# A hybrid encoder layer on one core: the layout of attention's queries, keys and outputs in DRAM

## The chip, the cores and the metric

The kernel runs on one core of a Trainium2 chip. Time is the device time of one execution in microseconds (us); the median of several runs counts. Beside the timed runs there is one profiled execution, from which every row shown here comes. Its engines: TensorE (PE) multiplies matrices, VectorE (DVE) and ScalarE (ACT) work on rows of 128 partitions, GpSimd (POOL) takes a few small operations and the accumulating transfers, SyncE (SP) issues all other transfers. A transfer (DMA) is moved by up to 16 transfer engines that all queues share.

## The reference

One layer over x (1024 frames of width 1024, float32). One projection gives queries, keys and values for attention (8 heads of 64), forget gates, the inputs of a gated linear recurrence (4 heads of 128) and two sets of merge gates. Then:

```python
y_a = fox_attention(q_a, k_a, v_a, log_fa)      # causal softmax(q k^T / 8 + F[t] - F[s]) v
y_b = rmsnorm(hgrn2_chunkwise(...)) * sigmoid(g_b)
merged = sigmoid(gate_a) * (y_a @ w_pa) + sigmoid(gate_b) * (y_b @ w_pb)
x = layer_norm(ALPHA * x + merged @ w_o)
x = layer_norm(ALPHA * x + (silu(g) * u) @ w_ff_out)   # u, g = split(x @ w_ff_in)
```

## The kernel before

**Precision and products.** A float32 operand is split into a high part (a cast to the fast type of TensorE) and a low part (the remainder). A product is three matmuls of these parts (`mm3`), each 128x128 by 128x512 as a rule. Most weight products are done two by two in Strassen's way: 7 block products in place of 8, with sums of blocks made on VectorE.

**Stages, in the order of time.** First the value projections and the forget gates (to about 90 us of the span). Then the steps in `ORDER`: "b" are pairs of projections for the recurrence, "q0" to "q3" make the queries and keys of two heads each (`qk_pair`), "r" are the recurrence's heads (`hgrn`), "e" and "g" the early and late parts of the merge gates (`gate_early`, `gate_late`), "a0" to "a7" the attention heads. Then the branch projections, the output projection, the first normalisation, the FFN in 22 chunks, and the second normalisation.

**Queries, keys and outputs on their way through DRAM.** `qk_pair` has a pair of heads in 128 partitions (64 of head 2p, 64 of head 2p+1) and stores four halves of them, high and low, in `qk_d[p, n]`: n = 0, 1 are the high and low parts of the queries, 2 and 3 those of the keys. There are 32 such stores of 128 rows of 2 KB. `qk_load` fetches what one head needs into three tiles of 128 partitions: `q2` holds the high queries in the upper 64 partitions and the low ones in the lower 64, `k2` the high keys twice, `kl` the low keys twice. A score is then two matmuls, `q2` with `k2` and `q2` with `kl`. Each tile is filled by two transfers of 64 rows of 4 KB, 48 in all. `attention` multiplies the probabilities with values that stand as high and low parts beside each other, so its result has the two parts' products in 2 x 64 partitions; it is stored in `ya_d[p, i]` (pair p, head i of it, part a), 16 stores. `branch_raw` brings the outputs of a pair of heads into one tile of 128 partitions: for each head a load of the first part by SyncE, and on it an accumulating transfer of the second part by GpSimd, 8 of each, 64 rows of 4 KB.

**Buffers.** Tiles are taken by tag; a tag has a fixed number of buffers, handed on in order. `ybox[0]` (the raw outputs) and `ybox[1]` (their sums for Strassen's products) take the tags "v" and "m", which before are the wide boxes of probabilities (`wide`) of the odd and the even heads, and later the two halves of the merged rows (`mraw`).

**What sets the order of the work.** All instructions are first recorded and then placed by a planner (`Plan`). It knows a cost for each operation (`cost`) and dependencies by tiles and by ranges of DRAM, simulates the engines and the transfers, and tries 36 variations of due times, of which it keeps the order with the earliest end. Each engine then runs its own instructions in that fixed order; so every constant of the planner can move instructions all over the kernel. For transfers it counts bytes at 235, 220 or 350 bytes per ns (64 rows, broadcast rows, others). An accumulating transfer is counted apart: it lands `LANDS` ns + bytes / `RATE` after its issue, and keeps the transfer engines for half of bytes / `RATE`. At most `RING` of them are under way.

Every operation is issued through one line of the planner (line 391), so the profile tells groups apart by tile names and not by lines. Names in rows: `qk_d`, `ya_d`, `part_d`, `gate_d` are in DRAM; `yboxv` is the raw outputs' tile and `yboxm` that of their sums before the change.

Of the kernel before, what the change touches and what calls it, by code (L numbers as in the profile page):

```python
# [7 lines left out]
F32 = mybir.dt.float32  # L8
# [4 lines left out]
ALU = mybir.AluOpType  # L13
# [3 lines left out]
P = 128  # L17
S = 1024
# [3 lines left out]
HA, DH = 8, 64  # L22
# [8 lines left out]
FIRST = 8  # L31
WARM = 7
ROUNDS = 36
ORDER = ("b10 00", "b20 21", "b11 01", "r0", "q0", "b12 02", "r1", "b22 23", "q1", "r2", "b13 03", "q2", "e0", "r3", "q3", "e1",
         "e2", "e3", "e4", "e5", "e6", "e7", "a0", "a1", "g0", "a2", "a3", "g1", "a4", "g2", "a5", "a6", "g3", "a7", "g4", "g5", "g6", "g7")
MARGIN = 1.06
SLACK = 400.0
SWITCH = 300.0
# [23 lines left out]
class Plan:  # L62
# [2 lines left out]

    LAT = {"PE": 197.0, "ACT": 131.0, "DVE": 128.0, "POOL": 66.0, "SP": 2400.0}
    OWN = {"PE": 0.0, "ACT": 0.0, "DVE": 127.0, "POOL": 60.0, "SP": 2400.0}
    SOFT, LANDS, RATE = 950.0, 1050.0, 190.0
    SETS = {AF.Exp: 0, AF.Ln: 0, AF.Sigmoid: 1, AF.Silu: 2}

    def __init__(self, tc):
# [68 lines left out]
    def cost(self, eng, method, outs, ins, kw):  # L140
        o = outs[0]
        n = o.free_size()
        psum = any(str(a.space).endswith("PSUM") for a in ins)
        if eng == "PE":
            dt = ins[0].dtype
            if method == "transpose":
                return 109.0
            if dt == F32:
                return 2 * max(112.0, n / 1.2 + 2)
            return n / 2.4 + 13.4 if n > 128 else 111.0  # L150
        if eng == "ACT":
            d = n / 1.2 + (52 if psum else 94) + 95 * (o.partition_size() == DH)
            if "accum_out" in kw:
                d += 93
            return d + 93 * sum(isinstance(kw.get(x), bass.AP) for x in ("scale", "bias"))
        if eng == "DVE":
            scal = sum(1 for a in ins if a.free_size() == 1 and n > 1)
            two = method in ("tensor_scalar", "tensor_copy") and not psum
            if method == "reciprocal":
                return 90.0  # L160
            if method == "tensor_tensor_scan":
                return n * 2.1 + 69
            if method == "copy_predicated":
                return n * 1.3 + 69
            if method == "bn_stats":
                n = ins[0].free_size()
            return n * (0.5208 if two else 1.0417) + 69 + 61 * min(scal, 2)
        if eng == "POOL":
            if method == "dma_start":
                return self.SOFT  # L170
            if method == "tensor_tensor" and kw.get("op") == ALU.pow:
                return 500 + 260 * n
            if method == "tensor_scalar":
                return n * 0.833 + 244
            return n * 2.35
        near = ins[0] if str(o.space).endswith("DRAM") else o
        rate = 235.0 if near.partition_size() == DH else 220.0 if ins[0].ap[0][0] == 0 else 350.0
        return float(o.nbytes()) / rate

    def kind(self, call):  # L180
# [2 lines left out]
    def schedule(self, slack, wait):  # L183
# [13 lines left out]
        dma_free = 0.0  # L197
# [18 lines left out]
        while done < len(calls):  # L216
            best = None
            for q, av in avail.items():
                for i in av:
                    t = max(free[q], ready[i])  # L220
                    ok = True
                    need = {}
                    for name in calls[i][6]:
# [10 lines left out]
                        t = max(t, sorted(slots[tag])[k][0] + 60)  # L234
# [3 lines left out]
                    if self.lands[i]:  # L238
                        t = max(t, ring[-RING])
                    if q == "SP":  # L240
                        t = max(t, under_way[-8])
# [8 lines left out]
            t, _, i, q = best  # L250
            c = calls[i]
            avail[q].remove(i)
            d = c[7] * (1 if q in ("PE", "SP") else MARGIN)
# [3 lines left out]
            if q == "SP":  # L257
                start = max(t + 100, dma_free)
                dma_free = start + d
                free[q] = t + 480  # L260
                fin = dma_free
                under_way.append(fin + self.LAT["SP"])
            else:
                if q == "ACT":
                    kind = self.kind(c)
                    if kind is not None and kind != table:
                        table = kind
                        t -= wait
                        d += 1283
                free[q] = t + d  # L270
                fin = t + d + self.lands[i]
                if self.lands[i]:
                    fin += max(0.0, dma_free - t - d)
                    dma_free = max(dma_free, t + d) + 0.5 * (self.lands[i] - self.LANDS)
                    fin = max(fin, ring[-1] + self.lands[i] - self.LANDS)
                    ring.append(fin)
            self.times[i] = t
# [117 lines left out]
def trunk(ctx: ExitStack, tc, a: dict, out: bass.AP):  # L395
    nc = tc.nc
    plan = Plan(tc)
    sync, act, dve, pool, pe = (plan.queue(n, e) for n, e in (
        ("SP", nc.sync), ("ACT", nc.scalar), ("DVE", nc.vector), ("POOL", nc.gpsimd), ("PE", nc.tensor)))
# [4 lines left out]
    dram = ctx.enter_context(tc.tile_pool(name="dram", bufs=1, space=DRAM))  # L404
# [12 lines left out]
    def take(tag, shape, name, dt=F32):  # L417
        return plan.tile(root, [P] + shape, dt, tag, name, BUFS[tag])
# [20 lines left out]
    def hs(i):  # L439
        return slice(i * NB, (i + 1) * NB)  # L440
# [4 lines left out]
    def f(ap):  # L445
        return ap.bitcast(F32)
# [79 lines left out]
    def block(k, n, tags, name):  # L526
        return [take(tag, [2, NB], f"{name}_{i}", F32) for i, tag in enumerate(tags)], a["w_v"][k, n]
# [6 lines left out]
    def rows(b):  # L534
        return [b[0][c // 2][:, c % 2, :] for c in range(4)]

    xa = take("m", [KC, NB], "xa_r")
    b11 = block(0, 0, ("kb", "kb"), "b11")
# [15 lines left out]
    for k, b, A, p, o in ((0, b11, A11, "p1", vx), (1, b21, A12, "p2", vy)):  # L554
        T = stationary4("v" + p)
        raw = rows(b)
# [18 lines left out]
    b12 = block(0, 1, ("qk", "qk"), "b12")  # L575
    b22 = block(1, 1, ("qk", "qk"), "b22")
# [126 lines left out]
    b22 = block(1, 1, ("hl", "hl"), "b22_2")  # L703
# [13 lines left out]

    ya_d = dram.tile([4, 2, 2, DH, S], F32, name="ya_d")

    v_d = dram.tile([HA, P, NT, 2, DH], F32, name="v_d")  # L720
    for h in range(HA):
        two = take("qk", [NT, 2, DH], f"v{h}", F32R)
        split(two[:, :, 0, :], two[:, :, 1, :], va[:, :, h * DH:(h + 1) * DH])
        sync.dma_start(v_d[h], f(two))

    qk_d = dram.tile([4, 4, P, S], F32, name="qk_d")
    lanes = [0]
    scored = []

# [66 lines left out]
    def qk_pair(p, raws, banks):  # L796
        name = f"qk{p}"

        def put(b, hf, o, sv):
            hi, lo = (half("gt" if n else "tt", f"{name}_{b}{hf}{n}", F32R) for n in range(2))  # L800
            if b == 0:
                act.activation(hi, o, AF.Copy, scale=-0.125)
                dve.scalar_tensor_tensor(lo, o, -0.125, f(hi), op0=ALU.mult, op1=ALU.subtract)
            else:
                split(hi, lo, o)
            for n, t in enumerate((hi, lo)):
                sync.dma_start(qk_d[p, 2 * b + n, :, hs(hf)], f(t))

        strassen_pair(name, [a["w_qk"][b, p] for b in range(2)], raws, banks, False, put)

# [75 lines left out]

    def qk_load(h):
        p, i = divmod(h, 2)
        me = slice(i * DH, (i + 1) * DH)
        q2, k2, kl = full("qk", f"q2_{h}", F32R), full("kb", f"k2_{h}", F32R), full("kb", f"kl_{h}", F32R)  # L890
        for t, ns in ((q2, (0, 1)), (k2, (2, 2)), (kl, (3, 3))):
            for j, n in enumerate(ns):
                sync.dma_start(f(t)[j * DH:(j + 1) * DH], qk_d[p, n, me])
        return q2, k2, kl

    def attention(h):
        p, i = divmod(h, 2)
        if True:
            plan.behind = tuple(scored[:max(h - 1, 0)][-1:])
            q2, k2, kl = qk_load(h)  # L900
# [11 lines left out]
            for qb in range(NT):  # L912
                n = (qb + 1) * P
# [40 lines left out]
                g = qb // 4  # L954
# [12 lines left out]
                    mm(pv[:, off:], vj, tl[:, off:], start=False, stop=j == qb)  # L967
                y = half("gt", f"ya{h}_{g}")
                act.copy(y, pv)
                sync.dma_start(ya_d[p, i].rearrange("a d t -> (a d) t")[:, hs(g)], y)  # L970


    ones = keep([P, P], "once", F32R)
    raw = half("gt", "once_r")[:, :P]
# [152 lines left out]
    pairs = 0  # L1127
    for step in ORDER:
        kind, n = step[0], int(step[1])
# [18 lines left out]

    ZTAGS = ["kb"] * 4 + ["hl"] * 2 + ["qk"] * 2
    YTAGS = ["qk"] * 4 + ["pf"] * 4  # L1150
    ybox = [take(t, [4, S], f"ybox{t}") for t in "vm"]
    def operand(tag, name):
        t = take(tag, [2, 4, NB], name, F32R)
        return t[:, 0], t[:, 1]
# [20 lines left out]
    def branch_raw(i, c):  # L1175
        if i:
            return raw_load(yb_d[c], [S], f"yr{i}{c}")
        raw = ybox[0][:, c]
        for n in range(2):
            for j in range(2):  # L1180
                o = raw[j * DH:(j + 1) * DH]
                if n:
                    pool.dma_start(o, ya_d[c, j, n], accum_op=ALU.add)
                else:
                    sync.dma_start(o, ya_d[c, j, n])
        return raw

    def gated(i, fb, hf):
# [16 lines left out]
    for c in range(2):  # L1205
# [4 lines left out]
        t = y24[c]  # L1210
# [20 lines left out]
    for n in range(KC // 2):  # L1231
        raw = raw_load(a["w_p"][0, n], [2, 4, P], f"wp0_{n}", n % 2)
        b11, b21, b12, b22 = raw[:, 0, :2], raw[:, 0, 2:], raw[:, 1, :2], raw[:, 1, 2:]
# [38 lines left out]
    for i in (1,):  # L1272
        yh, yl = [], []
        for c in range(4):
            raw = branch_raw(i, c)
# [3 lines left out]
        for fb in range(KC):  # L1279
# [5 lines left out]
            for hf in range(2):  # L1285
                sg = gated(i, fb, hf)
                o = bank(CYC[nbank % 5], f"pps{i}_{fb}_{hf}")
# [397 lines left out]
    for k, o, T in zip(ks, banks, T3s):  # L1685
        product(o[2], T, S4, False)
        dve.tensor_add(k.u2, o[2], k.u2)
        a0 = ring(f"ar{k.c}_0")
        dve.tensor_mul(a0, k.u2, k.sl)
        activations(k.c, a0, k.a1)  # L1690
    for c in range(2, FC):
        if c in (14, 17):
            hf = c // 17
# [44 lines left out]
    for prod in ("p1", "p5", "p6", "p4", "p7", "p2"):  # L1738
# [3 lines left out]
        for g in range(len(GR)):  # L1742
            d, n = group(prod, ai[prod], g)
# [4 lines left out]
        for t in range(4):  # L1748
            o = acc[t]
# [29 lines left out]
    for t in range(4):  # L1779
# [5 lines left out]
        for i, s_ in enumerate(parts):  # L1785
            w = s_.stop - s_.start
            o = next_bank(f"p3_{t}_{i}")
# [107 lines left out]
```

## Time and profile before

| | |
|---|---|
| Median of 3 runs | 1408.17 us (1407.49 to 1409.93) |
| Profiled execution: its time / its span | 1405.97 / 1404.1 us |
| Mean granted clock of TensorE | 0.996 |
| Busy: PE, DVE, ACT, POOL | 1386.7, 1151.3, 659.3, 97.6 us |
| Moved by transfers | 252.5 MB, 180 GB/s over the span |

A profile row of a group of instructions names engine, operation, the tile written and the tiles read (out<-in), shapes, and the number of instructions. A row of a transfer ends with the KB of one and the median time in us from issue to landing. In a table of stretches each engine has its busy time and, in brackets, its instructions; the last three columns are the granted clock, the mean busy share of the 16 transfer engines and GB/s. In a timeline the columns are start and duration in us, and in square brackets the idle time before an instruction with what ended it. TensorE's matmuls are pipelined: one of 128x512 shows a duration of about 390 ns, while the next starts 227 ns after it.

### The profile page before, as it was taken

How to read it: one execution, taken by the hardware profiler on the slowest of the kernel's cores; microseconds unless marked ns; L12 is line 12 of the kernel's file. 1: busy time of each engine (PE TensorE's matmuls, PEld its weight loads, DVE VectorE, ACT ScalarE, POOL GpSimd, SP SyncE). 2: the span in 40 equal slices, each digit the busy share in tenths (PEclk: the TensorE clock that was granted, in tenths of full speed). 3: DMA queues.
4: the chain of work that ended last, by engine and by line, in shares of the span. 5: the costliest groups of instructions: out<-in, count | busy, mean ns of one | idle time of the engine just before them, and what ended most of it. 6: DMA issues, size and time to landing. Idle time of an engine off the chain costs nothing.

```text
span 1404.1 us, 19027 instructions
## 1 busy us (share of the span) xinstructions
PE 1386.7 (99%) x6578; PEld 1150.8 (82%) x6578; DVE 1151.3 (82%) x2026; ACT 659.3 (47%) x1207; POOL 97.6 (7%) x112
## 2 busy tenths in 40 slices
PE   9999999999999999899999999999999999999997
PEld 7788888888888888688887888888888888888886
DVE  8998898887589896798998889877687966888596
ACT  6545454444577575465549832233322334434330
POOL 0000100000124242000001000000000000000011
PEclk9999999999999999999999999999999999999999
DMA  7134343448899966756544636532224337977632
GB/s 273 38 148 160 105 136 128 158 150 277 263 305 295 265 201 189 232 173 224 196 150 135 218 108 225 170 120 101 95 105 135 113 113 234 356 254 231 216 118 83
DMA packets 104255, 252.51 MB, mean 180 GB/s; under 512 B 11984, under 2 KB 17232, under 8 KB 104160
## 3 DMA queue, kind: packets, MB, share of 16 engines
q1 hardware_dynamic: 102368, 245.01, 53.0%
q0 software_dynamic: 1792, 6.29, 2.3%
q8 instruction: 52, 0.85, 0.2%
q14 instruction: 43, 0.35, 0.1%
HBM read 184.87 MB, written 66.39 MB: 179 GB/s over the span
## 4 chain that ended last, share of the span: by engine, by line
PE 95%; DMA 3%; DVE 1%; issue 0%; ACT 0%; SPq 0%; DVEq 0%; ACTq 0%
PE p L391 15%; PE fb L391 12%; PE fc L391 9%; PE gl_h L391 6%; PE fa L391 5%; PE b_h L391 4%; PE b_s L391 4%; PE vx L391 4%; PE fe L391 3%; PE oa L391 3%; PE pps L391 3%; PE ge L391 3%; PE qk_s L391 3%; PE qk_h L391 3%; PE vy L391 3%; PE ob L391 2%
## 5 line engine op out<-in xcount | busy, mean ns | idle before, releaser
L391 PE MATMUL p<-dp 128*128 128x512 f32 (+1 forms) x957 | 210.1, 382 | 0.0
L391 PEld LDWEIGHTS p<-dp 128*128 128x128 f32 x957 | 175.1, 188 | 34.8
L391 PE MATMUL fc<-xs,Tp 128*128 128x512 f32 x528 | 128.9, 389 | 0.0
L391 PE MATMUL fb<-xs,Tp 128*128 128x512 f32 x528 | 127.8, 389 | 0.0
L391 PEld LDWEIGHTS fb<-xs,Tp 128*128 128x128 f32 x528 | 99.1, 188 | 20.6
L391 PEld LDWEIGHTS fc<-xs,Tp 128*128 128x128 f32 x528 | 99.1, 188 | 20.6
L391 ACT CAST Tp<-t 128x512 fp32r<-128x512 f32 x88 | 54.4, 620 | 127.7 <-PE fb L391 66.1
L391 DVE TENSOR_TENSOR Tp<-t,Tp 128x512 fp32r<-128x512 f32 x88 | 60.3, 688 | 29.8 <-ACT Tp L391 29.4
L391 PE MATMUL fa<-x,Tp 128*128 128x512 f32 x336 | 81.2, 389 | 0.0
L391 PEld LDWEIGHTS fa<-x,Tp 128*128 128x128 f32 x336 | 63.1, 188 | 13.1
L391 POOL TENSOR_TENSOR norm<-norm,few 128x1 f32<-128x1 f32 x16 | 13.5, 843 | 802.1 <-DVE norm L391 794.0
L391 ACT CAST dp<-dap 128x1024 fp32r<-128x1024 f32 (+1 forms) x42 | 41.0, 979 | 52.8 <-PE p L391 29.0
L391 DVE TENSOR_TENSOR dp<-dap,dp 128x1024 fp32r<-128x1024 f32 (+1 forms) x42 | 47.4, 1130 | 17.6 <-ACT dp L391 15.7
L391 DVE TENSOR_TENSOR tl<-pt,th 128x512 fp32r<-128x512 f32 (+1 forms) x96 | 52.5, 552 | 8.6 <-ACT th L391 4.5
L391 ACT CAST th<-pt 128x512 fp32r<-128x512 f32 (+1 forms) x96 | 45.7, 477 | 25.9 <-PE pt L391 22.9
L391 PE MATMUL fb<-x,Tp 128*128 128x512 f32 x240 | 57.6, 389 | 0.0
L391 PEld LDWEIGHTS fb<-x,Tp 128*128 128x128 f32 x240 | 45.0, 188 | 9.4
L391 DVE TENSOR_TENSOR u<-fb,p 128x512 f32<-128x512 f32 x40 | 27.6, 689 | 22.0 <-PE fb L391 21.9
L391 POOL TENSOR_SCALAR p_w<-p_w,sums 128x640 f32<-128x640 f32 (+3 forms) x32 | 37.7, 1203 | 36.0 <-DVE sums L391 36.0
L391 ACT CAST Tp<-wg_r 128x512 fp32r<-128x512 f32 x28 | 17.5, 623 | 47.1 <-PE fb L391 25.4
L391 ACT CAST dp<-chain 128x1024 fp32r<-128x1024 f32 (+1 forms) x18 | 17.7, 982 | 42.0 <-issue 21.5
L391 DVE TENSOR_TENSOR u<-fc,u 128x512 f32<-128x512 f32 x44 | 30.1, 685 | 7.1 <-PE fc L391 7.1
(1657 smaller groups left out, 3685.0 us busy)
## 6 DMA issues: line engine op xcount, KB each, us to landing
dbp<-in_w_fo SPq DMA_DIRECT2D x45, 512.0 KB, 4.8
dap<-a_d SPq DMA_DIRECT2D x35, 512.0 KB, 4.5
wg_r<-in_w_ff SPq DMA_DIRECT2D x22, 512.0 KB, 4.1
wu_r<-in_w_ff SPq DMA_DIRECT2D x22, 512.0 KB, 3.7
a_d<-ar SPq DMA_DIRECT2D x42, 256.0 KB, 3.2
wop_r<-in_w_o SPq DMA_DIRECT2D x18, 512.0 KB, 4.0
a_d<-as SPq DMA_DIRECT2D x33, 256.0 KB, 3.2
qk_d<-qk SPq DMA_DIRECT2D x32, 256.0 KB, 3.9
```

What stands on the lines that cost most here:

```text
L391: getattr(q.engine, method)(*args, **kw)
```

## The change

1. `qk_d` is laid out as [pair, head, part, 64 rows, frame] in place of [pair, part, 128 rows, frame]. The stores still take 128 partitions; their DRAM side is now two heads of 64 rows that lie apart. `q2` is loaded in one transfer of 128 rows that lie one after the other. `k2` and `kl` are loaded in one transfer each, whose source names the 64 rows twice (a leading dimension of step 0 and size 2, `rows`).
2. `ya_d` is stored as [pair, part, head, row, frame] and not [pair, head, part, row, frame], so the two heads of one part lie one after the other. `branch_raw` takes one load and one accumulating transfer of 128 rows for a pair of heads. The stores' DRAM side is two parts of 64 rows that lie apart.
3. `ybox[0]` takes "m" and `ybox[1]` takes "v".
4. In the planner an accumulating transfer lands 1950 ns + bytes / 238 after its issue and keeps the transfer engines for all of bytes / 238. The rate of broadcast rows is used only where the leading dimension has step 0 and size 128.
5. `ORDER` is another: "b13 03" before "r2", "e1" before "q3", "g0" and "g1" one attention head earlier.

```diff
-ORDER = (... "r1", "b22 23", "q1", "r2", "b13 03", "q2", "e0", "r3", "q3", "e1",
-         "e2", "e3", "e4", "e5", "e6", "e7", "a0", "a1", "g0", "a2", "a3", "g1", "a4", "g2", "a5", "a6", "g3", ...)
+ORDER = (... "r1", "b22 23", "q1", "b13 03", "r2", "q2", "e0", "r3", "e1", "q3", "e2", "e3",
+         "e4", "e5", "e6", "e7", "a0", "g0", "a1", "a2", "g1", "a3", "a4", "g2", "a5", "a6", "g3", ...)
...
-    SOFT, LANDS, RATE = 950.0, 1050.0, 190.0
+    SOFT, LANDS, RATE = 950.0, 1950.0, 238.0
...
-        rate = 235.0 if near.partition_size() == DH else 220.0 if ins[0].ap[0][0] == 0 else 350.0
+        rate = 235.0 if near.partition_size() == DH else 220.0 if tuple(ins[0].ap[0]) == (0, P) else 350.0
...
-                    dma_free = max(dma_free, t + d) + 0.5 * (self.lands[i] - self.LANDS)
+                    dma_free = max(dma_free, t + d) + self.lands[i] - self.LANDS
...
+    def rows(ap, n=1):
+        return bass.AP(tensor=ap.tensor, offset=ap.offset, ap=[[0, n]] * (n > 1) + [list(d) for d in ap.ap])
...
-    qk_d = dram.tile([4, 4, P, S], F32, name="qk_d")
+    qk_d = dram.tile([4, 2, 4, DH, S], F32, name="qk_d")
...
-                sync.dma_start(qk_d[p, 2 * b + n, :, hs(hf)], f(t))
+                sync.dma_start(qk_d[p, :, 2 * b + n, :, hs(hf)], f(t))
...
-        me = slice(i * DH, (i + 1) * DH)
...
-        for t, ns in ((q2, (0, 1)), (k2, (2, 2)), (kl, (3, 3))):
-            for j, n in enumerate(ns):
-                sync.dma_start(f(t)[j * DH:(j + 1) * DH], qk_d[p, n, me])
+        sync.dma_start(f(q2), qk_d[p, i, :2].rearrange("n d t -> (n d) t"))
+        for t, n in ((k2, 2), (kl, 3)):
+            sync.dma_start(f(t), rows(qk_d[p, i, n], 2))
...
-                sync.dma_start(ya_d[p, i].rearrange("a d t -> (a d) t")[:, hs(g)], y)
+                sync.dma_start(ya_d[p, :, i, :, hs(g)], y)
...
-    ybox = [take(t, [4, S], f"ybox{t}") for t in "vm"]
+    ybox = [take(t, [4, S], f"ybox{t}") for t in "mv"]
...
-        for n in range(2):
-            for j in range(2):
-                o = raw[j * DH:(j + 1) * DH]
-                if n:
-                    pool.dma_start(o, ya_d[c, j, n], accum_op=ALU.add)
-                else:
-                    sync.dma_start(o, ya_d[c, j, n])
+        sync.dma_start(raw, ya_d[c, 0].rearrange("j d t -> (j d) t"))
+        pool.dma_start(raw, ya_d[c, 1].rearrange("j d t -> (j d) t"), accum_op=ALU.add)
```

More of the change, by code (lines that the diff above doesn't have):

```diff
@@ L33 @@
 ROUNDS = 36
-ORDER = ("b10 00", "b20 21", "b11 01", "r0", "q0", "b12 02", "r1", "b22 23", "q1", "r2", "b13 03", "q2", "e0", "r3", "q3", "e1",
-         "e2", "e3", "e4", "e5", "e6", "e7", "a0", "a1", "g0", "a2", "a3", "g1", "a4", "g2", "a5", "a6", "g3", "a7", "g4", "g5", "g6", "g7")
+ORDER = ("b10 00", "b20 21", "b11 01", "r0", "q0", "b12 02", "r1", "b22 23", "q1", "b13 03", "r2", "q2", "e0", "r3", "e1", "q3", "e2", "e3",
+         "e4", "e5", "e6", "e7", "a0", "g0", "a1", "a2", "g1", "a3", "a4", "g2", "a5", "a6", "g3", "a7", "g4", "g5", "g6", "g7")
 MARGIN = 1.06
```

## The prediction

> **What bounds the kernel now.** I read the page first, then TensorE's waits, the timeline around the one long wait, the chain of waits there, and last the transfers. The page and the waits of TensorE:
>
> ```profile
> span 1404.1 us, 19027 instructions
> PE 1386.7 (99%) x6578; PEld 1150.8 (82%) x6578; DVE 1151.3 (82%) x2026; ACT 659.3 (47%) x1207; POOL 97.6 (7%) x112
> PE 95%; DMA 3%; DVE 1%; issue 0%; ACT 0%; SPq 0%; DVEq 0%; ACTq 0%
> ...
> PE gl_h L391 <- DVE gl_b L391: 6.6, 1, 6.6
> PE vy L391 <- DVE idle L391: 1.2, 1, 1.2
> PE pv L391 <- ACT ya L391: 0.5, 1, 0.5
> PE s L391 <- DMA kl<-qk_d: 0.4, 1, 0.4
> ```
>
> TensorE is busy for 1386.7 of 1404.1 us. No edit here adds or removes a matmul, so what can be won is idle time, and most of the part that transfers cause is one wait of 6.6 us. Its neighbourhood, from the timelines of TensorE and of the issuing queue and from the chain:
>
> ```profile
> 567.09 0.39 PE L391 MATMUL gl_h<-xh,Tgl6p1l 128*128 128x512 f32 x1
> 574.11 0.79 PE L391 MATMUL gl_h<-xh,Tgl6p2h 128*128 128x512 f32 x1 [6.63 <-DVE gl_b L391]
> 574.70 0.63 PE L391 MATMUL gl_h<-xl,Tgl6p2h 128*128 128x512 f32 x1
> ...
> 577.90 0.40 PE L391 MATMUL gl_h<-xh,Tgl6p2h 128*128 128x512 f32 x1
> ...
> 548.02 2.37 SPq L391 DMA_DIRECT2D yboxv<-ya_d  x4
> ...
> 555.62 16.45 DMA gl_b<-part_d
> ...
> 682.39 10.88 PE oa L391 x48
> ```
>
> A gate's partial product takes 16.45 us to come in, behind the loads of attention's outputs that begin at 548.02; DVE's add waits for it, and so does the bank that TensorE wants. The nine matmuls from 574.11 to 577.90 take 3.8 us, where the plain distance of 0.227 us (10.88 us for 48 in the last row) would make 2.0: 1.7 us more. So the wait costs 6.8 + 1.7 = 8.5 us, and with the 0.4 and 0.5 us that hang on a load and on an eviction about 9.
>
> The transfers have a second story. Two full stretches, then the two in which queries and keys are written and read:
>
> ```profile
> 471.00:474.00 3.00, 3.00 (x19) 2.50 (x18) 2.56 (x5) 2.11 (x4) 0.64 (x1) 1.00 1.02 413
> 498.00:501.00 3.00, 3.00 (x22) 2.61 (x21) 2.92 (x11) 1.79 (x5) 0.60 (x1) 1.00 1.02 212
> 260.00:360.00 100.00, 100.00 (x520) 85.10 (x519) 75.59 (x133) 47.97 (x108) 7.34 (x6) 1.00 0.67 211
> 360.00:562.00 202.00, 200.76 (x1100) 169.67 (x1099) 162.67 (x468) 134.87 (x301) 66.71 (x77) 1.00 0.85 252
> ```
>
> The last two columns are the busy share of the 16 transfer engines and GB/s. At the same share of 1.02 one stretch moves 413 GB/s and the other, which follows six 64-row loads, 212. So a 64-row load takes about twice the engine time of its bytes, and the attention stage fills the engines to 0.85. That is the room the change aims at, and also the reason why transfer time is scarce exactly there.
>
> **The change part by part.** The moved transfers, counted from 260 to 562 us:
>
> ```profile
> qk_d<-qk SPq DMA_DIRECT2D x23, 256.0 KB, 5.8
> q<-qk_d SPq DMA_DIRECT2D x16, 256.0 KB, 9.0
> vhl<-v_d SPq DMA_DIRECT2D x8, 512.0 KB, 4.7
> k<-qk_d SPq DMA_DIRECT2D x16, 256.0 KB, 6.1
> kl<-qk_d SPq DMA_DIRECT2D x16, 256.0 KB, 7.4
> ya_d<-ya SPq DMA_DIRECT2D x15, 256.0 KB, 7.6
> ```
>
> All have 128 rows afterwards, but not of one kind. The query load and the loads of the outputs merge into one run of 128 rows, like `vhl<-v_d`. The key loads read 64 rows twice: their source pattern begins with a dimension of two (stride 0). The stores of queries, keys and outputs write a pattern that begins with two as well (two heads, then 64 rows). The trace of before has no transfer that begins with two. It has one whose pattern is shorter than 16, and single transfers of 128 rows to set beside it (the packets of three short windows, each with that one transfer):
>
> ```profile
> DMA packets 16, 0.02 MB, mean 11 GB/s; under 512 B 8, under 2 KB 8, under 8 KB 16
> ...
> f_d<-fs SPq DMA_DIRECT2D x1, 16.0 KB
> ...
> DMA packets 144, 0.52 MB, mean 308 GB/s; under 512 B 16, under 2 KB 16, under 8 KB 144
> q1 hardware_dynamic: 144, 0.52, 75.3%
> ...
> DMA packets 144, 0.26 MB, mean 238 GB/s; under 512 B 16, under 2 KB 16, under 8 KB 144
> q1 hardware_dynamic: 144, 0.26, 62.4%
> ```
>
> The small packets are the completion marks, one for each transfer engine that took part: 16 for 128 rows (88.9 to 90.6 us and 521.1 to 522.2 us), but 8 for the store of eight rows (60.2 to 61.7 us). I read it so: a transfer is dealt out along its first dimension, and a first dimension below 16 uses fewer engines. For the changed key loads and stores the count therefore lies between 2 and 16. Nearest is the row with eight, which had as many engines as its first dimension: I take 2 and keep 16 as the other end.
>
> [...]
>
> Prices. One 128-row load of 512 KB keeps each engine for 0.753 x 1.7 = 1.28 us, eight rows of 4 KB, 0.16 us a row; a store of 256 KB for 0.624 x 1.1 = 0.69 us, 0.086 us a row of 2 KB. On two engines each takes 64 rows: 64 x 0.16 = 10.2 us for a key load, 64 x 0.086 = 5.5 us for a store. All of it falls on the same two engines, and every other transfer has a sixteenth of its rows on those, so it ends when they get to it.
>
> The sum for these two engines from 260 to 562 us, 302 us long:
> - work before: 0.67 x 100 + 0.85 x 202 = 238.7 us;
> - taken out: 38 stores x 0.69 = 26.2, and 48 loads of 0.262 MB at 212 GB/s, 1.24 us each, 59.4; left 153.1;
> - put in: 38 stores x 5.5 = 209.0, 16 key loads x 10.2 = 163.2, 8 query loads x 1.28 = 10.2, together 382.4.
>
> That is 535.5 us of work in 302 us, so this stretch grows by 233 us, and TensorE waits with it: the score matmuls wait for keys, the gates for weights and partial products. The nine earlier stores (172 to 260 us) go into idle transfer time and cost nothing; without that cover it would be at most 9 x 5.5 = 50 us. The work after 562 us has to queue behind, so nothing is given back.
> Bounds: if the other 49.5 MB (72.0 moved in the window, less 10.0 and 12.6) ran at 413 GB/s, 120 us in place of 153, it is 502 us, 200 more than before. If the two engines were filled to 0.85 only, as all are now, 535.5/0.85 = 630 us, 328 more.
> [...]
>
> Buffers: the raw outputs take the even heads' box (tag m) in place of the odd heads' (v). The loads at 548.02 come just after the odd head's last read; the even heads end earlier, so they can begin earlier. In exchange the first half of the merged rows, first written at 609.8, waits for the box of the sums:
>
> ```profile
> L391 PE MATMUL pt<-ident,p_w x208: 270/272/329, 386.3 to 547.7; 128*128 128x128 f32 x104
> ...
> L391 DVE TENSOR_TENSOR ys<-yboxm,ys x5: 684/684/1215, 587.3 to 602.2; 128x512 fp32r<-128x512 f32 x4, 128x1024 fp32r<-128x1024 f32 x1
> ...
> L391 DVE TENSOR_TENSOR m<-pu,sg x8: 681/683/691, 609.8 to 644.3; 128x512 f32<-128x512 f32 x8
> ```
>
> That box is last read about 603, 6 us before: cost nothing; without that margin the wait would show whole on DVE. One accumulation for each pair of heads in place of two takes 4 issues off GpSimd, which is 7% busy. ORDER and the three constants move instructions only; with everything spread over 16 engines this is worth between -9 us (the waits above gone) and +8 us (one more such wait, 6.8 + 1.7).
>
> Sum: 1404.1 + 233 + 0 = 1637 us of span; the profiled execution took 1.9 us more than its span and lay 2.2 us under the median shown, so 1642 us.
>
> **The rivals.**
> *Spread over 16, faster.* If a leading dimension of two is dealt out over all engines, transfers need 153.1 + 26.2 + 24 x 1.28 = 210 us where they needed 239, and the outputs come in earlier; the 16.45 us load shortens and the wait goes: 1408 - 9 = 1399 us. For it: the 212 beside 413 GB/s, and the outputs' load starting 0.3 us after its buffer came free. Against it: the eight marks of the store of eight rows.
> *Spread, no difference.* The wait moves to another partial product: 1408.
> *Spread, slower.* An accumulation is now 512 KB, counted in full by the planner, and a partial product is put behind it a second time: 8 us, 1416. It decides where a load lands over 6 us late, as the one of 16.45 us did.
> *Key loads alone.* The stride-0 pattern is confined and the stores are not: 153.1 + 26.2 + 163.2 + 10.2 = 353 us in 302, 51 us more, 1459.
>
> **How the numbers follow.** Two engines for loads and stores 0.62, loads alone 0.06, spread and faster 0.17, spread without difference 0.07, spread and slower 0.08. I don't go higher with the first, since the trace shows a short pattern of eight, not one of two with 64 rows behind it. 0.2% (2.8 us) is about what a measurement of this kernel tells from no change: faster 0.17, same 0.07, slower 0.62 + 0.06 + 0.08 = 0.76. The forecast's own range is 1560 to 1740: up to the upper bound (1408 + 328), and below the lower (1608) because loads may be issued ahead of need. It holds 0.56 alone, so the range goes on down to 1398, just under the faster case.
>
> **What would show it.** Right: between about 260 and the end of attention TensorE is no longer 99% busy but idles in many places on the loads of `k`, `kl` and the gates' weights; key loads land after 10 us at the least, stores of `qk_d` after 5.5; the mean busy share of the transfer engines falls although the stage waits for them; few completion marks for each transfer. The stages after it are as long as before. Wrong: key loads of 512 KB that land in 4 to 5 us as `vhl` does, a span of attention near 190 us, and a time under 1420 us; then the question is only whether the wait at 567 us is gone.

## The result and the profile after

The changed kernel takes 1657.47 us (median of 4, 1656.18 to 1659.42), the kernel before 1408.06 beside it (1407.49 to 1409.93): a ratio of 1.177, 95% interval 1.1749 to 1.179. The profiled execution took 1658.49 us with a span of 1656.6, 252.5 us more than before.

The page of the changed kernel (busy time, transfers, chain of waits by engine) and TensorE's waits:

```profile
span 1656.6 us, 18996 instructions
...
PE 1441.7 (87%) x6578; PEld 1183.2 (71%) x6578; DVE 1152.2 (70%) x2026; ACT 659.5 (40%) x1207; POOL 91.5 (6%) x108
...
DMA packets 102848, 252.51 MB, mean 152 GB/s; under 512 B 10576, under 2 KB 15824, under 8 KB 102752
...
PE 52%; DMA 18%; issue 3%; DVE 3%; SPq 2%; ACT 2%; POOL 0%; DVEq 0%; ACTq 0%; POOLq 0%
...
PE pt L391 <- DVE tl L391: 49.7, 3, 25.2
PE pt L391 <- POOL p L391: 33.1, 3, 23.3
PE pv L391 <- ACT th L391: 20.3, 3, 7.8
PE s L391 <- DMA q<-qk_d: 18.3, 2, 15.2
```

The bytes and the matmuls are those of before. Transfers have 18% of the chain in place of 3%, TensorE 52% in place of 95%. TensorE's own waits name attention's DVE, GpSimd and ScalarE before any transfer; only the chain shows what these were late for. Some of its long pieces in attention, in order of time (start, duration, what), and what GpSimd does in the longest of them:

```profile
399.54 21.07 DMA qk_d<-qk
...
466.00 13.99 DMA part_d<-ge
...
507.90 18.51 DMA q<-qk_d
...
588.66 28.46 issue
...
683.79 23.57 DMA ya_d<-ya
...
773.40 18.56 DMA sg<-gate_d
...
617.14 0.90 POOL L391 DMA_DIRECT2D box<-nf_d  x1 [28.48 <-DMA box<-in_causal]
```

Stores of the new pattern stand there, and beside them transfers that the change doesn't touch (`part_d`; `sg` from `gate_d`): these are late too. The piece called "issue" is GpSimd waiting 28.48 us for a mask (`box` from `in_causal`, which the change doesn't touch either) before it can issue an accumulating transfer; the `p` that TensorE waits for up to 23.3 us stands behind that in GpSimd's order. Where the time lies, by stretches (columns as in the prediction: length, busy time of each engine, granted clock, share of the 16 transfer engines, GB/s), first of the kernel before, then of the changed one:

```profile
172.00:260.00 88.00, 88.00 (x474) 75.52 (x473) 78.31 (x134) 41.14 (x84) 3.06 (x3) 1.00 0.40 135
260.00:562.00 302.00, 300.76 (x1619) 254.76 (x1618) 238.26 (x600) 182.84 (x408) 74.05 (x83) 1.00 0.79 239
...
580.00:1404.10 824.10, 815.80 (x3656) 674.04 (x3654) 673.21 (x1015) 339.37 (x537) 14.30 (x17) 1.00 0.51 168
```

```profile
172.00:260.00 88.00, 79.32 (x387) 65.67 (x386) 62.01 (x110) 34.50 (x73) 3.57 (x3) 0.96 0.33 110
260.00:813.70 553.70, 362.06 (x1709) 296.68 (x1708) 262.69 (x635) 193.68 (x425) 67.61 (x80) 0.82 0.43 139
...
832.00:1656.60 824.60, 811.17 (x3617) 668.04 (x3615) 664.19 (x1002) 335.91 (x532) 13.50 (x16) 0.99 0.50 167
```

Up to 172 us (170.82 us of TensorE in both), and over the last 824 us, the two are alike. Attention's last product with values is at 562 us before and at 813.7 us after; between 260 us and that point lie 302 us before and 553.7 us after. Between these stretches lie 18.0 us before (562 to 580) and 18.3 us after (813.7 to 832). The mean share of the transfer engines fell from 0.79 to 0.43 in the stretch that waits for transfers. What a mean of 0.43 hides shows in a stretch with one key load and nearly nothing else (373.55 to 384.0 us), and in one in the middle of one store (177.65 to 179.65 us); the packets of both, and the queue's share of the first:

```profile
DMA packets 131, 0.53 MB, mean 51 GB/s; under 512 B 2, under 2 KB 2, under 8 KB 130
...
q1 hardware_dynamic: 130, 0.52, 12.5%
...
DMA packets 50, 0.10 MB, mean 51 GB/s; under 512 B 0, under 2 KB 0, under 8 KB 50
```

The key load leaves two completion marks, keeps 12.5% of 16 engines busy, which is two, and needs some 10.1 us for its 512 KB. The store runs at the same 51 GB/s and keeps 13.4% of 16 engines busy, so it has two as well and takes 256 KB / 51 = 5.1 us. No profile here names an engine, but that these transfers share one pair shows in time. SyncE's issues (start, duration, what), then the packets from 373.55 to 392.3, from 392.3 to 394.6 and from 394.6 to 396 us:

```profile
371.11 0.54 SPq L391 DMA_DIRECT2D k<-qk_d  x1
377.06 0.51 SPq L391 DMA_DIRECT2D kl<-qk_d  x1
391.34 0.33 SPq L391 DMA_DIRECT2D box<-in_causal  x1
...
DMA packets 238, 0.97 MB, mean 52 GB/s; under 512 B 2, under 2 KB 2, under 8 KB 237
...
DMA packets 150, 0.55 MB, mean 239 GB/s; under 512 B 16, under 2 KB 16, under 8 KB 150
...
DMA packets 22, 0.07 MB, mean 47 GB/s; under 512 B 2, under 2 KB 2, under 8 KB 22
```

The second key load is issued at 377.06, while the first is under way and 14 engines are idle (12.7% of 16 are busy up to 392.3 us). Still the rate stays at 52 GB/s up to 392.3 us: it waits for the first one's pair. Then comes the mask, a load over all 16 engines. Up to 394.6 us there are 16 marks, the second key load's two and 14 of the mask's; the mask's last two come after that, at the 47 GB/s of two engines. So the other 14 engines ran ahead, and the mask, spread over all 16, ended when the pair got to its share. Two stores of the new pattern, issued from 391.77 on, wait as well: from 394.6 to 396 us everything together moves 47 GB/s, and from 396 to 398 us 51.

### The profile page after: what moved, and what is told of

It is laid out like the page before. It is cut to its first block, busy times and chain, and to the rows that moved or that the text cites. A ratio compares the mean times of both kernels' runs of the same rounds, so it can differ in the third digit from the quotient of the medians.

```text
span 1656.6 us, 18996 instructions
## 1 busy us (share of the span) xinstructions
PE 1441.7 (87%) x6578; PEld 1183.2 (71%) x6578; DVE 1152.2 (70%) x2026; ACT 659.5 (40%) x1207; POOL 91.5 (6%) x108
## 4 chain that ended last, share of the span: by engine, by line
PE 52%; DMA 18%; issue 3%; DVE 3%; SPq 2%; ACT 2%; POOL 0%; DVEq 0%; ACTq 0%; POOLq 0%
PE p L391 12%; PE fb L391 11%; PE fc L391 7%; PE fa L391 5%; PE gl_h L391 3%; DMA qk_d<-qk 3%; DMA ya_d<-ya 3%; DMA part_d<-ge 3%; PE oa L391 3%; DMA wg<-in_w_g 2%; DMA sg<-gate_d 2%; PE ob L391 2%; DMA gate_d<-gl_b 2%; SPq L391 2%; PE fe L391 2%
## 5 line engine op out<-in xcount | busy, mean ns | idle before, releaser
L391 PE MATMUL pt<-ident,p 128*128 128x128 f32 x80 | 17.7, 318 | 57.7 <-POOL p L391 33.1
L391 PE MATMUL pt<-ident,p_w 128*128 128x128 f32 x208 | 38.1, 293 | 32.5 <-DVE tl L391 25.2
L391 PE MATMUL s<-k,q 128*128 128x512 f32 (+3 forms) x96 | 36.5, 389 | 30.6 <-DMA q<-qk_d 18.3
L391 PEld LDWEIGHTS pt<-ident,p_w 128*128 128x128 f32 x208 | 28.0, 150 | 40.8 <-DVE tl L391 26.8
L391 PEld LDWEIGHTS pt<-ident,p 128*128 128x128 f32 x80 | 11.6, 161 | 62.2 <-POOL p L391 34.6
L391 PE MATMUL pv<-th,vhl 128*128 128x512 f32 (+1 forms) x96 | 35.8, 373 | 20.4 <-ACT th L391 20.3
```

Source lines behind the costliest of these rows:

```text
L391: getattr(q.engine, method)(*args, **kw)
```

## The experiments

**Which part costs the time: all three patterns spread, and each of them alone left as changed.** The first variant keeps the change's merged transfers, buffers, constants and order, and only lets every pattern begin with 64 or 128 rows:

```diff
-    qk_d = dram.tile([4, 2, 4, DH, S], F32, name="qk_d")
+    qk_d = dram.tile([4, P, 4, S], F32, name="qk_d")
...
+    def twice(ap, step):
+        d = [list(x) for x in ap.ap]
+        return bass.AP(tensor=ap.tensor, offset=ap.offset, ap=[d[0], [step, 2]] + d[1:])
...
-                sync.dma_start(qk_d[p, :, 2 * b + n, :, hs(hf)], f(t))
+                sync.dma_start(qk_d[p, :, 2 * b + n, hs(hf)], f(t))
...
-            sync.dma_start(f(t), rows(qk_d[p, i, n], 2))
+            sync.dma_start(f(t), twice(qk_d[p, i * DH:(i + 1) * DH, n], 0))
...
-    ya_d = dram.tile([4, 2, 2, DH, S], F32, name="ya_d")
+    ya_d = dram.tile([4, P, 2, S], F32, name="ya_d")
...
-                sync.dma_start(ya_d[p, :, i, :, hs(g)], y)
+                sync.dma_start(ya_d[p, :, i, hs(g)], y)
...
```

`twice` gives the pattern [rows, 2 at this step, frames]. The query load names each row of 64 with its high and low part in the same way, and the outputs' rows come in as (row, head), for which the rows of the branch's weights stand in that order. The other three are this variant with one pattern as in the change: key loads (`rows(..., 2)`), stores of queries and keys, stores of outputs.

> The changed kernel with all its transfers of 128 rows, its buffers, its planner constants and its ORDER, but each transfer's pattern begins with 64 or 128 on both sides: queries and keys stand in DRAM as (head, row, part), so a store has 128 rows of one step, and a head's loads deal the rows out in the order (row, part) in place of (part, row); the outputs stand as (part and row, head). The order of the rows in a tile changes for q2, k2 and kl alike, and for the outputs the rows of the branch weight are laid out to match. Theory (two engines for a pattern that begins with two): the two busiest engines then have 153 + 38 x 0.69 + 24 x 1.28 = 210 us of work in the 302 us of the stage, so the loss is gone: 1399 to 1416 us, and every transfer has 16 completion marks (the total of small packets rises by 64 x 14 = 896 over the changed kernel's 10576). Rival (the planner's constants and ORDER brought the loss): they are all still in, so 1600 us or more.

> As the run with every pattern spread, but the two key loads of a head read their 64 rows twice with the leading dimension of two, as in the change; the query load is two transfers of 64 rows, as before the change. Theory: 153 + 38 x 0.69 + 16 x 10.2 + 16 x 1.24 = 362 us of work on two engines in 302 us: 60 us more than before, 1468 us. Should only the stores be confined and not the loads with step 0: as the spread run. Rival (planner and ORDER): 1600 us or more.

> As the run with every pattern spread, but queries and keys stand in DRAM as the change has them, so the 32 stores begin with two; the loads of queries and keys are dealt out in the order (row, part) and begin with 64. Theory: 23 stores from 260 us on take 23 x 5.5 = 126 us on two engines in place of 16; over the whole stage 153 + 126 + 10 + 31 = 321 us in 302, 19 us more, but they come within 100 us, where 50 us of other work stands too: 76 us more if nothing of it drains under attention. 1427 to 1484 us, nearest 1455. Rival (planner and ORDER): 1600 us or more.

> As the run with every pattern spread, but attention's outputs are stored with two parts of 64 rows that lie apart, as in the change. Theory: 16 stores x 5.5 = 88 us on two engines, 153 + 83 + 16 + 31 = 283 us of work in 302: nearly covered, 1405 to 1425 us. Rival (planner and ORDER): 1600 us or more.

| | us (median) | ratio to before, 95% interval |
|---|---|---|
| all spread | 1405.38 | 0.9967, 0.9956 to 0.9979 |
| key loads on two | 1538.89 | 1.0919, 1.0897 to 1.0941 |
| stores of queries and keys on two | 1480.74 | 1.0507, 1.0486 to 1.0528 |
| stores of outputs on two | 1435.16 | 1.0183, 1.0163 to 1.0204 |
| all on two (the change) | 1657.47 | 1.177, 1.1749 to 1.179 |

The three variants with one pattern on two are medians of two runs each. The packets of the four variants, in the order of the table:

```profile
DMA packets 103744, 252.51 MB, mean 180 GB/s; under 512 B 11472, under 2 KB 16720, under 8 KB 103648
```

```profile
DMA packets 103648, 252.51 MB, mean 164 GB/s; under 512 B 11376, under 2 KB 16624, under 8 KB 103552
```

```profile
DMA packets 103296, 252.51 MB, mean 171 GB/s; under 512 B 11024, under 2 KB 16272, under 8 KB 103200
```

```profile
DMA packets 103521, 252.51 MB, mean 176 GB/s; under 512 B 11249, under 2 KB 16497, under 8 KB 103425
```

With all spread there are 11472 small packets, 896 = 64 x 14 more than in the changed kernel: 64 transfers (32 + 16 stores, 16 key loads) with 16 marks in place of 2. The single variants have 96, 448 and 223 fewer than that. Two of these are the patterns' own: 32 x 14 = 448 and 16 x 14 = 224 (223 by these rows, which count all queues; on the queue that carries these stores it is 224: 101920 packets against 101696). The first isn't: 16 key loads would make 224 fewer, but this variant loads its queries by two transfers per head, 8 transfers of 16 marks more, 128: 224 - 128 = 96.

The loss goes away with the patterns and comes back with each. Beyond the spread variant the three cost 133, 75 and 30 us, 238 together, and all at once 252. The first of these also has its query loads in 16 transfers of 64 rows in place of 8 of 128, so the 133 us aren't the key loads' alone. In the key-load variant TensorE waits like this:

```profile
PE pv L391 <- ACT th L391: 35.9, 4, 14.4
PE s L391 <- DMA q<-qk_d: 25.6, 1, 25.6
...
412.26 16.71 SPq L391 DMA_DIRECT2D part_d<-ge  x1
...
443.00:448.00 5.00, 0.00 (x0) 0.00 (x0) 0.00 (x0) 0.00 (x0) 0.00 (x0) 0.50 0.13 52
```

The longest wait, up to 452.71 us, is for a query load, spread over all engines. SyncE issues it only at 431.38, since the issue of a store before it, at 412.26, took 16.71 us; and from 443 to 448 us two engines alone are busy, at 52 GB/s: the load ended when the pair got to its share. All three variants came out above what I had expected (1468; 1455 as the nearest of 1427 to 1484; 1405 to 1425). I had taken the work of a whole stage against its whole length; but the work only comes from the time on when these transfers start. The stretch that is really stretched, in each variant (key loads, stores of queries and keys, stores of outputs):

```profile
318.00:701.60 383.60, 269.94 (x1338) 224.45 (x1337) 198.29 (x532) 158.52 (x352) 64.08 (x77) 0.83 0.57 168
...
k<-qk_d SPq DMA_DIRECT2D x8, 512.0 KB
kl<-qk_d SPq DMA_DIRECT2D x8, 512.0 KB
```

```profile
260.00:461.00 201.00, 153.10 (x710) 124.52 (x709) 103.72 (x192) 65.86 (x143) 11.26 (x11) 0.88 0.43 138
...
qk_d<-qk SPq DMA_DIRECT2D x23, 256.0 KB
```

```profile
390.00:592.00 202.00, 180.41 (x969) 150.51 (x968) 155.64 (x433) 124.00 (x274) 53.88 (x66) 0.95 0.71 230
...
ya_d<-ya SPq DMA_DIRECT2D x15, 256.0 KB
```

Work of the pair = (share x length - 2/16 of the confined work) + the confined work. Key loads: 0.57 x 383.6 = 218.7, less 20.4, plus 16 x 10.2 = 163.2: 361 of 384 us, 94%. Stores of queries and keys: 86.4 - 15.8 + 126.5 = 197 of 201, 98%. Stores of outputs: 143.4 - 10.3 + 82.5 = 216 of 202, 107%, or 104% at the 5.1 us measured for one store. So within the accuracy of such shares (the two full stretches of the kernel before, 471 to 474 and 498 to 501 us, show 1.02, and the stretches were chosen with the result at hand) the pair is full in all three.

**The dose: four engines in place of two.** The spread variant, with the outputs stored as four runs of 32 rows:

```diff
-    ya_d = dram.tile([4, P, 2, S], F32, name="ya_d")
+    ya_d = dram.tile([4, 4, 2, 32, S], F32, name="ya_d")
...
-                sync.dma_start(ya_d[p, :, i, hs(g)], y)
+                sync.dma_start(ya_d[p, :, i, :, hs(g)], y)
...
```

> As the variant with all three patterns dealt out row by row, but the sixteen stores of attention's outputs write a pattern that begins with four (four runs of 32 rows) where the change has two. Theory (the number of engines is the leading dimension, and a stage is stretched once those engines are full): 4 completion marks for each of these stores, so 11472 - 16 x 12 = 11280 small packets; a store keeps each of its four engines for 32 rows x 0.086 = 2.75 us, 15 of them 41 us. Between 380 and 592 us each engine had 152.7 - 10.3 = 142 us of work beside them; 142 + 41 = 183 us in 212 is 87% full, so there is room: about 1405 to 1412 us, where the same stores on two engines cost 27 us more than none. Rival A (a pattern with the rows in the second dimension is slow by itself, however many engines it has): the same as with two, about 1432 us, or half of it, 1419. Rival B (cost grows with the work on the engines in proportion, full or not): half of 27, 1419 us.

It took 1415.45 us (1412.88 to 1416.81), 1.0042 of the kernel before (1.0028 to 1.0057). Its packets, and the stretch in which the stores lie:

```profile
DMA packets 103552, 252.51 MB, mean 179 GB/s; under 512 B 11280, under 2 KB 16528, under 8 KB 103456
...
390.00:560.00 170.00, 164.87 (x918) 138.23 (x917) 146.51 (x418) 118.69 (x265) 55.45 (x66) 0.99 0.78 259
```

The number of marks is the expected 11280: four engines. The time is 10 us over the spread variant, one third of what two engines cost, where I had expected 0 to 7. The cost fell with the number of engines (30 us with two, 10 with four), so Rival A in its full form is out; that it costs anything at all I put down to a stretch chosen too long again. From 390 to 560 us the four engines have 0.78 x 170 - 10.3 + 41.3 = 163.6 us of work in 170, 96%: hardly any room. Rival B's 1419 lies 1.7 us above the interval's upper end (1.0057 x 1409.24 = 1417.3), which is close; this run alone doesn't put it away. The four doses together, though they lie in different stretches, speak for a room that is used up first: confined work beyond its even share of 31, 72, 111 and 143 us (41.3 x 12/16, then 82.5, 126.5 and 163.2 x 14/16) cost 10, 30, 75 and 133 us, so 0.3, 0.4, 0.7 and 0.9 us for each us.

**The rest of the change: buffers, constants, order.** Four variants of the kernel before: with buffers, constants and order but the old layout; with the spread layout alone; with the buffers alone; with constants and order alone. The buffers' edit is one line:

```diff
-    ybox = [take(t, [4, S], f"ybox{t}") for t in "vm"]
+    ybox = [take(t, [4, S], f"ybox{t}") for t in "mv"]
```

> The kernel before, with its old layout and all its transfers of 64 rows, and of the change only the buffers of the raw outputs and their sums, the planner's counting of accumulating transfers and the order of the stages. Theory (nothing of the loss comes from these; the prediction put them at between -9 and +8 us): 1399 to 1416 us, and, as the accumulations are still eight of 64 rows, likely within 3 us of the kernel before, with a wait on a gate's partial product of about 6 us or none. Rival (order and constants carry a good part of the 249 us, the layouts only bringing it out): 1430 us or more.

> The spread layout (all patterns begin with 64 or 128 rows, transfers merged as in the change) with the kernel before's order of stages, buffers and planner constants. Theory (what the spread variant won, about 3 us, came from merged transfers that take 16 engines): 1403 to 1408 us, as the spread variant. Rival (the 3 us came from the order, the buffers and the constants): 1408 to 1412 us here, and 1404 to 1406 us in the run that has those alone.

> The kernel before with one edit: the raw outputs take the even heads' box and their sums the odd heads'. Theory (the buffers are what won 0.33% in the run of buffers, order and constants: there the first loads of outputs began at 531 us in place of 548, so the gates' partial products no longer queue behind them): the loads of outputs begin near 531 us, the wait of 6.6 us on a partial product is gone, 1403 to 1406 us. Rival (order and constants won it): within 1.5 us of the kernel before, about 1408 us, with the wait still there or moved to another partial product.

> The kernel before with the order of stages and the planner's counting of accumulating transfers of the change, but the old buffers and the old layout. Theory (the buffers won the 0.33%): the loads of outputs still begin near 548 us, 1407 to 1411 us. Rival (order and constants won it): 1403 to 1406 us.

| | us (median) | ratio to before, 95% interval |
|---|---|---|
| buffers, constants, order | 1404.54 | 0.9967, 0.9952 to 0.9982 |
| spread layout alone | 1404.95 | 0.9968, 0.9955 to 0.998 |
| buffers alone | 1403.02 | 0.9961, 0.9946 to 0.9975 |
| constants and order alone | 1409.74 | 1.001, 1.0001 to 1.0019 |

No part of the 249 us is here. The buffers alone have the lowest time of the study, though the intervals of the first three overlap; the run with all of the rest lies 4.7 us below the kernel before, where I had expected it within 3. The issuing queue's first loads of outputs (start, duration, what) and TensorE's wait for a gate's partial product, buffers alone first, then constants and order alone:

```profile
528.73 1.73 SPq L391 DMA_DIRECT2D yboxm<-ya_d  x3
...
PE gl_h L391 <- DVE gl_b L391: 0.6, 1, 0.6
```

```profile
555.64 2.37 SPq L391 DMA_DIRECT2D yboxv<-ya_d  x4
...
PE gl_h L391 <- DVE gl_b L391: 4.6, 1, 4.6
```

In the even heads' box the loads begin 19 us earlier than at 548.02, and TensorE's wait for a partial product is down from 6.6 to 0.6 us. With constants and order alone they begin later still, and the wait stays, at 4.6 us.

Do the buffers' gain and the layout's add up? The spread layout with the new buffers, old order and constants:

> The kernel before with the spread layout and the changed buffers, but the old order and constants. If the two gains (0.39% of the buffers, 0.32% of the layout) came from different losses, they add up: about 1398 us. If both only take away the one wait of 6.6 us on a partial product, they don't: 1402 to 1406 us. I expect the second, since the buffers alone leave TensorE waiting for transfers nowhere.

1408.23 us, 0.9996 (0.9986 to 1.0006): not only no sum, but neither of the gains. Its longest TensorE wait, the chain there, and ScalarE's timeline:

```profile
PE pv L391 <- ACT th L391: 5.8, 1, 5.8
...
533.12 14.44 DMA sg<-gate_d
...
547.64 0.63 ACT L391 ACTIVATE sg<-sg 128x512 f32<-128x512 f32 x1 [7.21 <-DMA sg<-gate_d]
```

A load of a stored gate takes 14.44 us, ScalarE stands 7.21 us at the sigmoid that needs it, and behind that sigmoid stands attention's `th` (548.68 us). The wait of 6.6 us is gone and another of 5.8 us is in its place. So gains of 0.3% here depend on which transfer the planner happens to put behind which, and I don't assign them to the layout.

## Why the prediction was right, and where its steps were off

*The number of engines* was right: two, by marks, by the 12.5%, and by a key load of 10.1 us where 10.2 was forecast. A store takes 5.1 us by its rate, where 5.5 was forecast. "Key loads alone", and the three rivals in which the chip spreads such a pattern, are out: stores confine too. That all such transfers fall on the same two engines no row of before showed; the changed kernel shows it, with 52 GB/s while a second key load stood behind the first. The price of 51 us for key loads alone came from the whole stage and was far too low; with the split query loads they cost 133 us.

*The sum* forecast +233 us, and the span grew by 252.5. With the rows of the changed kernel the pair had, from 260 to 813.7 us, 0.43 x 553.7 = 238.1 us of mean work, of which the confined transfers' share is 2/16 of 366.7 (22 and 15 stores at 5.5, 16 key loads at 10.2), 45.8. Without it 192.3 remain, and 192.3 + 366.7 = 559 us of work in 553.7: the pair is full from end to end (with the 5.1 us measured for a store it is 546, 99%). The prediction had 153.1 + 10.2 = 163.3 in place of the 192.3, 29 us too few. Two things are in these 29 us. The stretch moved more than the 72.0 MB that the prediction counted:

```profile
DMA packets 28664, 76.75 MB, mean 139 GB/s; under 512 B 2573, under 2 KB 3597, under 8 KB 28636
```

The 4.7 MB more are 11 us at the 413 GB/s of the prediction's full stretch. And the 59.4 us taken out for 64-row loads, 1.24 us each, from one stretch of 3 us, were too much for a mean. The spread variant shows that, over the same 302 us, in which it moves the same 72.0 MB:

```profile
260.00:562.00 302.00, 297.13 (x1613) 249.58 (x1612) 247.56 (x608) 182.29 (x406) 68.33 (x80) 0.99 0.73 238
```

0.73 x 302 = 220 us, where the prediction made 210 for the same case, 10 too few. That accounts for 21 of the 29 us; the rest stays open. In the other direction, 37 stores at 5.5 in place of 5.1 us were 15 us too many, and 22 stores of queries and keys lie in the stretch, not 23. That the sum came as near as 233 to 252 is therefore in part luck. The recorded range from 1398 to 1740 us holds every rival too; its part from 1560 on is the one that only the two engines for loads and stores reach.

*The early stores* were to cost nothing between 172 and 260 us. That step was wrong. TensorE's busy time there fell from 88.00 to 79.32 us. With the same order and all patterns spread it is full:

```profile
172.00:260.00 88.00, 88.00 (x443) 74.25 (x443) 71.36 (x126) 42.19 (x86) 3.11 (x3) 1.00 0.43 140
```

So the change has 387 matmuls there in place of 443 (the 474 of the kernel before are those of another order). VectorE waited for the stores to free its tiles, and ScalarE too (5.2 and 4.6 us):

```profile
DVE qk L391 <- DMA qk_d<-qk: 6.6, 1, 6.6
```

The mean share of 0.40 was read as idle transfer time. On the mean there was room: the last two of the ten stores are issued at 257.55 and 259.16 us, the other eight are 8 x 5.1 = 41 us on the pair, and with 0.33 x 88 - 5 = 24 us beside them that is 65 of 88 us. But six of the eight are issued between 193.84 and 220.9 us, 31 us of work in 27. What this cost in the end isn't known, since the stretch behind it waits for the pair anyway.

*Nothing given back* was right: the last 824 us are as long as before.

*The buffers* were called free. They are worth 0.39% (0.25 to 0.54), 5.5 us, and the sign follows from the prediction's own remark that the loads can begin earlier. The wait they remove was priced at 8.5 us; it was worth 5.5. *Order and constants*, put between -9 and +8, are +0.1%. *Spread, faster* was put at 1399 us; the spread variant takes 1405.4, 0.33% less than before, and the run with layout and buffers shows that even this isn't the layout's for certain.

*The signs to look for* came as told, but two. TensorE's waits name attention's DVE, GpSimd and ScalarE first and not `k` and `kl`. And the page prints no landing times for the loads and stores of the new patterns, so these had to be read from packets; the chain has one key load, landing 13.33 us after its issue at 371.11.

Left open: why the three losses alone add up to 238 us and together make 252, how the price of confined work runs exactly below a full pair, and how much of the loss comes through long issues (last section).

## What to carry to other kernels

Count the completion marks of a transfer before its rows: 128 rows behind a leading dimension of two were a transfer on two engines here, at 51 GB/s, while 512 KB with 128 leading rows moved at 308 GB/s and 256 KB at 238 (88.9 to 90.6 and 521.1 to 522.2 us of the kernel before). Let the rows lead and put the repeat or the head behind them (`[rows, 2, frames]`); the same bytes and the same number of transfers then took 1405 us in place of 1657. A mean share of 0.43 hid a pair of engines that by the sum above was 99% full: add up the work of the pair, over the stretch in which it really comes.

## What the runs showed of the hardware that I had not expected

An issue itself took up to 14.8 us. Instructions of the issuing queue, min / median / max in ns, before and after, for a store that is spread over all engines (16 marks from 518.5 to 521 us before, where one of them runs alone) and that the change doesn't touch:

```profile
L391 SPq DMA_DIRECT2D gate_d<-gl_a x16: 319/320/1578, 403.9 to 603.5; - x16
```

```profile
L391 SPq DMA_DIRECT2D gate_d<-gl_a x16: 319/440/14808, 522.1 to 854.2; - x16
```

One store's issue took SyncE 14.8 us, where 1.6 us was the longest issue of any of its transfers before, and everything queued behind it, for all 16 engines, was issued later by that. In the queue's timelines from 290 us on, the longest issue that stands alone took 1.1 us with all patterns spread, but 16.7 us with the key loads on two, 5.2 us with the stores of queries and keys on two and 8.0 us with the stores of outputs on two. So long issues came with the two-engine patterns; that the full pair holds the issue back is my reading. And the granted clock fell with TensorE's idle time: 0.82 from 260 to 813.7 us, against 1.00 before. TensorE's busy time grew by 55 us (1386.7 to 1441.7) with the same matmuls.
